# Moving the S5 preparation of a hybrid trunk kernel to VectorE: broadcast products in pieces behind the weight splits

## The chip, the cores and the metric

The kernel runs on one core of one Trainium2 chip. The metric is the device time of one execution in microseconds (us); the kernel before takes 1494.66 us, the median of three runs. A core has five engines that run their own queues of instructions: TensorE (PE in the profile) multiplies matrices, VectorE (DVE) and GpSimd (POOL) work elementwise, ScalarE (ACT) applies functions and copies, and SyncE (SP) issues the transfers (DMA).

## The reference

`reference.py` computes two layers on 272 tokens (16 learned ones and 256 of x) with 1024 features, all in float32. What matters here is the frame and head group D, the S5 state space:

```python
for l in range(DEPTH):
    h = h + 0.5 * swiglu(rms_norm(h, ffn1_norm[l]), ffn1_w_gate[l], ffn1_w_up[l], ffn1_w_down[l])
    h = h + hybrid_mixer(rms_norm(h, mix_norm[l]), w_in[l], w_out[l], lru_p, gdn_p, ssd_p, s5_p)
    h = h + 0.5 * swiglu(rms_norm(h, ffn2_norm[l]), ffn2_w_gate[l], ffn2_w_up[l], ffn2_w_down[l])
return rms_norm(h, final_norm)[:, N_META:]
...
def s5_mixer(u, a_re, a_im, log_dt, b_re, b_im, c_re, c_im, d_skip, w_glu, norm_g):
    mag = jnp.exp(dt * lam_re)
    ab_re = mag * jnp.cos(dt * lam_im)
    ab_im = mag * jnp.sin(dt * lam_im)
    f_re = ((ab_re - 1.0) * lam_re + ab_im * lam_im) / den
    f_im = (ab_im * lam_re - (ab_re - 1.0) * lam_im) / den
    bb_re = f_re[..., None] * b_re - f_im[..., None] * b_im
    bb_im = f_re[..., None] * b_im + f_im[..., None] * b_re
    bu_re = jnp.einsum("btgi,gpi->tbgp", ug, bb_re)
    ...
    _, _, s_re, s_im = lax.associative_scan(_complex_linear_combine, ...)
    y = jnp.einsum("tbgp,gip->btgi", s_re, c_re) - jnp.einsum("tbgp,gip->btgi", s_im, c_im)
```

Everything that depends on a, b, c and log_dt alone (no token) can be prepared ahead of the mixing sub-layer. That is the S5 preparation of which this document tells.

## The kernel before

**Stages.** Each layer is FFN1, mixing, FFN2. Activations have features on partitions and tokens on the free axis. The weights come in 382 chunks of 128 x 1024 numbers, 191 a layer: 66 for FFN1 (44 for gate and up, 22 for down), 59 for mixing, 66 for FFN2.

**A chunk's way.** SyncE loads it into `raw` (RAWS = 3 buffers); ScalarE makes its upper part `hi` (L214) and VectorE the lower part `lo` = raw - hi (L216; in mixing every fourth one on GpSimd); TensorE uses it in 24 matmuls, for each of eight 128 x 128 tiles hi x, hi x_lo and lo x (L227, L228, L229). `ahead` keeps AHEAD = 3 chunks split ahead of the one in use, in SPLITS = 4 buffers. In an FFN's gate and up part VectorE also does three operations of 128 x 272 for every two chunks (L353, L355, L358).

**What sets the order.** The program is written step by step, and a scheduler orders each engine's instructions by a simulated timeline in which code written earlier has priority, so that work whose inputs are there moves forward. An engine then executes its queue strictly in order.

**The S5 preparation.** The 16 pairs of S5 groups are treated in four quarters u of four pairs. `d_consts` makes the small arrays of both layers (a, its powers `pw`, the factor f). `d_powers(l, u)` multiplies b and c with f and the powers of a, as complex products `cmul` of 128 x 128 elements on GpSimd: eight products of six operations a quarter, and two more operations. `d_mats(l, u)` then makes four matrices with TensorE and ScalarE (transposes, F, H) and, on VectorE, tables of a ** (4 j) of 68 columns, in seven doubling steps of six small operations a quarter; all goes to DRAM (`spill`), and `d_load` brings it back in the mixing sub-layer. The scratch of `cmul` appears in the trace as dp (GpSimd) and cx (VectorE), the quarter's arrays as s5a, s5b, dU, du, rx and rg.

**Where it is called.** `run` gives each layer's FFN1 a table of hooks: after gate and up tile f = 1, 3, 7, 12, 16, 20 of 22 the quarters' powers and matrices; in layer 0, `mix_consts`, `a_consts` and `d_consts` (constants of the mixers, many small VectorE operations) come first, at f = 1. The second FFN has no hooks. As the powers of layer 1 depend on parameters alone, the scheduler moves them forward.

## Time and profile before

| | us |
|---|---|
| three runs | 1494.46, 1494.66, 1499.1 |
| median | 1494.66 |
| span of the profiled execution | 1506.5 |
| TensorE busy in it | 1407.3 |
| VectorE busy | 1078.3 |
| ScalarE busy | 698.3 |
| GpSimd busy | 536.1 |

The profiled execution is another one than the three that are timed; the page prints its span, from the first instruction to the last, and no time of its own beside it. Layer 0 has its FFN1 at about 12 to 244 us of the span, its mixing until about 570 and its FFN2 from about 605 to 800; layer 1 follows with FFN1 until about 1005, mixing until 1305 and FFN2 until 1495. PEclk is the granted TensorE clock, as a share of full speed.

### The profile page before, as it was taken

What the parts mean: (1) busy time and instruction counts of PE and PEld (TensorE: products, weight loads), DVE (VectorE), ACT (ScalarE), POOL (GpSimd) and SP (SyncE); (2) the same over time, 40 slices, a digit from 0 to 9 for tenths busy, and PEclk for the clock granted to TensorE, in tenths of its full rate; (3) what the DMA queues carried; (4) which work ended last, traced back from release to release, by engine and by line L of the source; (5) the groups of instructions that cost most, each with busy time, mean ns of one, the idle gap of its engine ahead of it and who ended that gap; (6) DMA issues with size and microseconds to landing.
All of it is one profiled execution on the core that took longest, in us unless ns stands there. A gap on an engine that the chain in (4) does not pass through costs nothing.

```text
span 1506.5 us, 28168 instructions
## 1 busy us (share of the span) xinstructions
PE 1407.3 (93%) x10838; PEld 1366.9 (91%) x10838; DVE 1078.3 (72%) x2078; ACT 698.3 (46%) x1169; POOL 536.1 (36%) x779
## 2 busy tenths in 40 slices
PE   7988999989898995999999999999898899999997
PEld 6987998979897895999999999998898879999997
DVE  8998666888987469556565876667898875666653
ACT  5435444444563342444444455443355633554442
POOL 2589312265544588000010660122564344200011
PEclk9999999989999997999999999999899989999998
DMA  6456664654422153555555667646454222565562
GB/s 222 149 192 210 235 227 139 203 192 114 134 78 90 43 170 107 185 169 178 173 179 159 201 206 252 210 137 209 137 172 134 85 85 70 165 199 184 185 188 88
DMA packets 85197, 243.18 MB, mean 161 GB/s; under 512 B 22968, under 2 KB 29896, under 8 KB 85064
## 3 DMA queue, kind: packets, MB, share of 16 engines
q1 hardware_dynamic: 85064, 241.38, 49.7%
q8 instruction: 86, 1.41, 0.4%
q14 instruction: 47, 0.39, 0.1%
HBM read 221.86 MB, written 19.49 MB: 160 GB/s over the span
## 4 chain that ended last, share of the span: by engine, by line
PE 65%; DVE 10%; POOL 2%; DMA 2%; issue 2%; ACT 1%; SPq 0%; DVEq 0%; ACTq 0%; POOLq 0%
PE g L227 18%; PE g L228 18%; PE g L229 18%; DVE lo L216 2%; PE m L664 2%; PE m L235 1%; PE m L257 1%; PE m L1143 1%; PE m L797 1%; DVE r L875 1%; DVE r L543 1%; PE m L1107 1%; DVE r L1112 1%; POOL lo L216 1%; DMA a<-scr 1%
## 5 line engine op out<-in xcount | busy, mean ns | idle before, releaser
L227 PE MATMUL g<-xh,hi 128*128 128x272 f32 (+1 forms) x2048 | 601.4, 294 | 46.2 <-DVE r L543 16.3
L214 ACT ACTIVATE hi<-raw 128x1024 fp32r<-128x1024 f32 (+1 forms) x382 | 402.4, 1054 | 471.1 <-PE g L228 230.3
L229 PE MATMUL g<-xh,lo 128*128 128x272 f32 (+1 forms) x2048 | 599.5, 294 | 14.2 <-DVE lo L216 14.1
L228 PE MATMUL g<-xl,hi 128*128 128x272 f32 (+1 forms) x2048 | 597.9, 293 | 1.4 <-DVE xl L312 1.4
L216 DVE TENSOR_TENSOR lo<-raw,hi 128x1024 fp32r<-128x1024 f32 (+1 forms) x352 | 454.1, 1290 | 202.5 <-ACT hi L214 199.9
L227 PEld LDWEIGHTS g<-xh,hi 128*128 128x128 f32 x2048 | 394.7, 193 | 49.0 <-issue 17.5
L229 PEld LDWEIGHTS g<-xh,lo 128*128 128x128 f32 x2048 | 393.8, 193 | 18.0 <-DVE lo L216 17.4
L228 PEld LDWEIGHTS g<-xl,hi 128*128 128x128 f32 x2048 | 394.6, 193 | 2.8 <-DVE xl L312 1.8
L272 POOL TENSOR_TENSOR acc<-acc,r 128x272 f32<-128x272 f32 (+1 forms) x42 | 44.2, 1052 | 515.7 <-ACT r L271 515.0
L216 POOL TENSOR_TENSOR lo<-raw,hi 128x1024 fp32r<-128x1024 f32 x30 | 74.5, 2482 | 82.7 <-ACT hi L214 82.6
L228 PE MATMUL g<-r,hi 128*128 128x272 f32 (+1 forms) x256 | 73.0, 285 | 0.0
L355 DVE TENSOR_TENSOR r<-r,g 128x272 f32<-128x272 f32 (+1 forms) x88 | 37.7, 429 | 36.7 <-PE g L229 34.9
L354 ACT ACTIVATE r<-r 128x272 f32<-128x272 f32 (+1 forms) x88 | 36.6, 416 | 46.4 <-DVE r L353 46.3
L229 PE MATMUL g<-ra,lo 128*128 128x272 f32 (+1 forms) x192 | 55.1, 287 | 0.0
L229 PE MATMUL g<-rq,lo 128*128 128x272 f32 (+1 forms) x192 | 55.0, 289 | 0.0
L227 PE MATMUL g<-ra,hi 128*128 128x272 f32 (+1 forms) x192 | 54.9, 286 | 0.0
L228 PE MATMUL g<-rs,hi 128*128 128x272 f32 (+1 forms) x192 | 54.9, 286 | 0.0
L228 PE MATMUL g<-rz,hi 128*128 128x272 f32 (+1 forms) x192 | 54.8, 285 | 0.0
L227 PE MATMUL g<-rq,hi 128*128 128x272 f32 (+1 forms) x192 | 53.8, 291 | 0.0
L353 DVE TENSOR_TENSOR r<-g,rstd 128x272 f32<-128x272 f32 (+1 forms) x88 | 38.0, 431 | 21.0 <-PE g L229 20.9
L249 POOL TENSOR_TENSOR toks<-tok,mhalf 128x2 f32<-128x2 f32 (+1 forms) x36 | 26.6, 752 | 70.9 <-DVE tok L246 65.1
L228 PEld LDWEIGHTS g<-r,hi 128*128 128x128 f32 x256 | 48.3, 189 | 0.0
(439 smaller groups left out, 2873.3 us busy)
## 6 DMA issues: line engine op xcount, KB each, us to landing
raw<-in_wgu_dram SPq DMA_DIRECT2D x176, 512.0 KB, 4.1
raw<-in_wdn_dram SPq DMA_DIRECT2D x88, 512.0 KB, 4.2
raw<-in_win_dram SPq DMA_DIRECT2D x80, 512.0 KB, 3.6
raw<-in_wout_dram SPq DMA_DIRECT2D x32, 512.0 KB, 3.5
spill<-s5a SPq DMA_DIRECT2D x8, 920.0 KB, 5.3
s5a<-spill SPq DMA_DIRECT2D x8, 920.0 KB, 4.7
s5b<-spill SPq DMA_DIRECT2D x8, 896.0 KB, 4.8
spill<-rx SPq DMA_DIRECT2D x4, 640.0 KB, 3.5
```

The costliest lines, as they stand in the source:

```text
L214: nc.scalar.activation(out=hi[:, 0:w], in_=raw[:, 0:w], func=AF.Copy)
L216: (nc.gpsimd if mixing and i % 4 == 1 else nc.vector).tensor_tensor(out=lo[:, 0:w], in0=raw[:, 0:w], in1=hi[:, 0:w].bitcast(F32), op=ALU.s ...
L227: nc.tensor.matmul(ps, lhsT=hi, rhs=xh, start=start, stop=False)
L228: nc.tensor.matmul(ps, lhsT=hi, rhs=xl, start=False, stop=False)
L229: nc.tensor.matmul(ps, lhsT=lo, rhs=xh, start=False, stop=stop)
L235: s.nc.tensor.matmul(ps[0:w, c + b * st:c + b * st + 1], lhsT=acc[:, o:o + w], rhs=s.ones[:, 0:1], start=True, stop=True)
L249: nc.gpsimd.tensor_tensor(out=rs[0:w, b0:b1], in0=tok[0:w, b0:b1], in1=s.mhalf[0:w, 0:1].to_broadcast([w, b1 - b0]), op=ALU.pow)
L272: (eng or nc.gpsimd).tensor_tensor(out=acc, in0=acc, in1=t, op=ALU.add)
L353: nc.vector.tensor_tensor(out=t, in0=g[:, t0], in1=r, op=ALU.mult)
L354: nc.scalar.activation(out=si, in_=t, func=AF.Silu)
L355: nc.vector.tensor_tensor(out=a, in0=si, in1=u[:, t0], op=ALU.mult)
L664: s.nc.tensor.matmul(ps[:, h * 128:h * 128 + 128], lhsT=lhs(h), rhs=rhs(h), start=True, stop=True)
```

## The change

The preparation becomes a generator, `d_prep(l)`, that yields after each small piece. `ahead` asks for one piece behind each weight split outside of mixing (from chunk 4 on), and the scheduler is told to place it behind that split. In layer 0's FFN1 the pieces are those of `d_consts`, `d_prep(0)`, `mix_consts` and `a_consts`, about 63 for 62 splits; `d_prep(1)` has 44 pieces, behind the splits of layer 0's FFN2, and layer 1's FFN1 has none. The rest, if any, is issued at the end of the FFN by `finish_work`.

In `d_prep`, the tables are made for all 16 pairs at once (seven steps of six operations of 16 to 512 columns a layer, in place of four times as many of 4 to 256). The products with b and c are four `twice` a quarter, each two products and a sum of 128 x 512 elements whose operands are broadcast: the powers of a up to the fourth come from a table `aux` that `d_consts` makes for both layers, of which layer 1's part waits in DRAM (`auxd`). All these are on VectorE; GpSimd keeps memsets. ScalarE takes over the copy of m4 and two copies into W. The tables are stored to DRAM apart, in eight small stores a layer, and their place in the quarter's array changes. The 8 transposes and 8 small matmuls of a quarter stay. The diff also drops comments, which moves line numbers.

```diff
@@ ahead
-            (nc.gpsimd if mixing and i % 4 == 1 else nc.vector).tensor_tensor(out=lo[:, 0:w], in0=raw[:, 0:w], in1=hi[:, 0:w].bitcast(F32), op=ALU.subtract)
+            ins = (nc.gpsimd if mixing and i % 4 == 1 else nc.vector).tensor_tensor(out=lo[:, 0:w], in0=raw[:, 0:w], in1=hi[:, 0:w].bitcast(F32), op=ALU.subtract)
             s.split.append((hi, lo))
+            if not mixing and i >= 4:
+                with s.tc.issue_after(ins.ins):
+                    next(s.work, None)
@@ ffn
-            for k in hooks.get(f, ()):
-                k()
@@ d_consts: many lines
...
+        for k in (3, 4):
+            rot(A(0, k), A(1, k), A(0, 2), A(1, 2), A(0, k - 2), A(1, k - 2))
+        yield
+        for k in (1, 2, 3):
+            rot(Fp(0, k), Fp(1, k), fr, fi, A(0, k), A(1, k))
...
+        nc.scalar.activation(out=s.aux, in_=aux[:, 0], func=AF.Copy)
+        nc.sync.dma_start(out=s.auxd, in_=aux[:, 1])
@@ cmul, d_powers and d_mats go
...
+    def twice(s, o, a, c, b, d, op, pat, **k):
+        v = s.nc.vector
...
+        t = s.pt(n).rearrange(pat, **k)
+        v.tensor_tensor(out=o, in0=a, in1=c, op=ALU.mult)
+        v.tensor_tensor(out=t, in0=b, in1=d, op=ALU.mult)
+        if n > 256:
+            yield
+        v.tensor_tensor(out=o, in0=o, in1=t, op=op)
+
+    def d_prep(s, l):
...
+        if l:
+            nc.sync.dma_start(out=s.aux, in_=s.auxd)
...
         for k in range(7):
             n = 1 << k
             m = min(n, NC4 - n)
...
+            yield from s.twice(tr[:, :, n:n + m], a, c, b, d, sub, 'p (q c) -> p q c', q=NQ)
+            if m > 4:
+                yield
+            yield from s.twice(ti[:, :, n:n + m], a, d, b, c, add, 'p (q c) -> p q c', q=NQ)
+            yield
+        for u in range(4):
...
+            for r, t in enumerate((tr, ti)):
+                nc.sync.dma_start(out=sp[:, 1296 + 272 * r:1568 + 272 * r], in_=t[:, qs, :].rearrange('p q c -> p (q c)'))
+            raw = s.buf('bc', [P, 4, 4, 32])
+            nc.sync.dma_start(out=raw, in_=s.ap['s5b'][l, u])
...
+            nc.scalar.activation(out=m4, in_=s.m4[:, l, qs].unsqueeze(2).to_broadcast([P, 4, NC4]), func=AF.Copy)
...
+            yield from s.twice(B[:, 0], over(0), fr, over(1), fi, sub, 'p (q k c) -> p q k c', **pat)
+            yield
+            yield from s.twice(B[:, 1], over(0), fi, over(1), fr, add, 'p (q k c) -> p q k c', **pat)
...
+            yield from s.twice(W[:, 0, :, 1:5], over(2), ar, over(3), ai, sub, 'p (q k c) -> p q k c', **pat)
+            yield
+            yield from s.twice(W[:, 1, :, 1:5], over(2), an, over(3), ar, sub, 'p (q k c) -> p q k c', **pat)
...
+    def first_work(s):
+        yield from s.d_consts()
+        yield from s.d_prep(0)
+        s.mix_consts()
+        yield
+        s.a_consts()
@@ run
-            hooks = {1: [lambda: s.d_powers(l, 0)], 3: [lambda: s.d_powers(l, 1)], 7: [lambda: s.d_mats(l, 0), lambda: s.d_powers(l, 2)],
-                     12: [lambda: s.d_mats(l, 1), lambda: s.d_powers(l, 3)], 16: [lambda: s.d_mats(l, 2)], 20: [lambda: s.d_mats(l, 3)]}
             if l == 0:
-                hooks[1] = [s.mix_consts, s.a_consts, s.d_consts] + hooks[1]
-            s.ffn(l, full, lambda m: s.norm_in(m, s.col('nm', l), full), hooks, l == 0)
+                s.work = s.first_work()
+            s.ffn(l, full, lambda m: s.norm_in(m, s.col('nm', l), full), l == 0)
+            s.finish_work()
...
+                s.work = s.d_prep(l + 1)
                 s.ffn(l, sl, lambda m: s.norm_in(m, s.col('n1', l + 1), sl))
+                s.finish_work()
```

**VectorE in layer 0's FFN1.** The rows are VectorE's queue in the gate and up part; lo is a weight split, r the FFN's activations, s5a the quarter's tables with their scratch cx, pw the powers of a, rx the products with c, rg the loaded b and c. Before:

```order
L1014 TENSOR_TENSOR cx_1078<-s5a_1045,pw 128x4x16
L1017 TENSOR_TENSOR cx_1078<-s5a_1045,pw 128x4x16
L914 TENSOR_TENSOR pw<-pw,a_72 128x32
L353 TENSOR_TENSOR r_1239<-g_1177,rstd 128x272
L914 TENSOR_TENSOR a_72<-pw 128x32
L914 TENSOR_TENSOR pw<-pw 128x32
L1013 TENSOR_TENSOR cx_1078<-s5a_1045,pw 128x4x16
L1018 TENSOR_TENSOR cx_1078<-s5a_1045,pw 128x4x16
L914 TENSOR_TENSOR pw<-pw,a_72 128x32
L1015 TENSOR_TENSOR s5a_1045<-cx_1078 128x4x16
L216 TENSOR_TENSOR lo_1236<-raw_1031,hi_1235 128x1024
L1019 TENSOR_TENSOR s5a_1045<-cx_1078 128x4x16
```

After the change:

```order
L217 TENSOR_TENSOR lo_1612<-raw_1520,hi_1611 128x1024
L1047 TENSOR_TENSOR rx_395<-rg_1444,aux 128x4x128
L1048 TENSOR_TENSOR cx_976<-rg_1444,aux 128x512
L360 TENSOR_TENSOR r_1621<-r_1620,g_1584 128x272
L217 TENSOR_TENSOR lo_1655<-raw_1561,hi_1654 128x1024
L1051 TENSOR_TENSOR rx_395<-rx_395,cx_976 128x4x128
L363 TENSOR_TENSOR r_1460<-r_1621,ra_1298 128x272
L358 TENSOR_TENSOR r_1692<-g_1627,rstd 128x272
L217 TENSOR_TENSOR lo_1687<-raw_1609,hi_1686 128x1024
L1047 TENSOR_TENSOR rx_395<-rg_1444,aux 128x4x128
```

The runs of small table operations between two splits are gone from here; behind each split stands one piece, two products of 128 x 512 or the sum of them.

**VectorE where layer 0's FFN2 begins.** The rows stand around the sums for the norm (tok); lo_6748 and lo_6531 are splits of the FFN's first chunks. Before, the tables of layer 1's first quarters stand here:

```order
L1017 TENSOR_TENSOR cx_9630<-s5a_9597,pw 128x4x32
L1018 TENSOR_TENSOR cx_9630<-s5a_9597,pw 128x4x32
L1015 TENSOR_TENSOR s5a_9597<-cx_9630 128x4x32
L246 TENSOR_SCALAR tok_6674<-m_6670 128x2
L246 TENSOR_SCALAR tok_6674<-m_6670 16x1
L1019 TENSOR_TENSOR s5a_9597<-cx_9630 128x4x32
L1013 TENSOR_TENSOR cx_9630<-s5a_9597,pw 128x4x4
L1014 TENSOR_TENSOR cx_9630<-s5a_9597,pw 128x4x4
L216 TENSOR_TENSOR lo_6748<-raw_6594,hi_6747 128x1024
L1017 TENSOR_TENSOR cx_9630<-s5a_9597,pw 128x4x4
L1018 TENSOR_TENSOR cx_9630<-s5a_9597,pw 128x4x4
L1015 TENSOR_TENSOR s5a_9597<-cx_9630 128x4x4
```

After the change:

```order
L1048 TENSOR_TENSOR cx_6406<-dz_973,aux 128x16
L302 SCALAR_TENSOR_TENSOR xl<-h,small,xh 128x272 x2
L1051 TENSOR_TENSOR dp_972<-dp_972,cx_6406 128x16
L277 TENSOR_TENSOR acc<-acc,r_6394 128x272
L1051 TENSOR_TENSOR dz_973<-dz_973,cx_6406 128x16
L251 TENSOR_SCALAR tok_6457<-m_6453 128x2
L251 TENSOR_SCALAR tok_6457<-m_6453 16x1
L217 TENSOR_TENSOR lo_6531<-raw_6367,hi_6530 128x1024
L1047 TENSOR_TENSOR dp_972<-dp_972,aux 128x16x2
L1048 TENSOR_TENSOR cx_6406<-dz_973,aux 128x32
L1047 TENSOR_TENSOR dz_973<-dp_972,aux 128x16x2
L1048 TENSOR_TENSOR cx_6406<-dz_973,aux 128x32
L1051 TENSOR_TENSOR dp_972<-dp_972,cx_6406 128x16x2
```

Here stand now the first pieces of `d_prep(1)`, whose tables are dp (real) and dz (imaginary).

**GpSimd at the end of layer 0's mixing.** The rows stand around the last sums of squares acc of the residual, which the norm ahead of FFN2 needs. Before, the powers of layer 1 (dp and rx, with abr and abi) stand between them:

```order
L1014 TENSOR_TENSOR dp_519<-rx_544,abr 128x4x32
L1013 TENSOR_TENSOR dp_519<-rx_544,abi 128x4x32
L272 TENSOR_TENSOR acc<-acc,r_6603 128x272
L1017 TENSOR_TENSOR dp_519<-rx_544,abr 128x4x32
L1018 TENSOR_TENSOR dp_519<-rx_544,abi 128x4x32
L1015 TENSOR_TENSOR rx_544<-dp_519 128x4x32
L272 TENSOR_TENSOR acc<-acc,r_6609 128x272
L1019 TENSOR_TENSOR rx_544<-dp_519 128x4x32
L1014 TENSOR_TENSOR dp_519<-rx_544,abr 128x4x32
L272 TENSOR_TENSOR acc<-acc,r_6615 128x272
L1013 TENSOR_TENSOR dp_519<-rx_544,abi 128x4x32
```

After the change:

```order
L217 TENSOR_TENSOR lo_6310<-raw_6247,hi_6309 128x1024
L1086 MEMSET s5b_6917 128x512
L1088 MEMSET s5a_6916 128x4
L277 TENSOR_TENSOR acc<-acc,r_6376 128x272
L277 TENSOR_TENSOR acc<-acc,r_6382 128x272
L277 TENSOR_TENSOR acc<-acc,r_6388 128x272
L254 TENSOR_TENSOR toks_6458<-tok_6457,mhalf 128x2
L254 TENSOR_TENSOR toks_6458<-tok_6457,mhalf 16x1
L1140 MEMSET dz_973 128x4 x2
L1088 MEMSET s5a_7252 128x4
```

GpSimd has memsets and the norm's own operations here.

## Rows read from the trace of the kernel before

**Rows 1.** The page: span, then busy time, share and count by engine.
```profile
span 1506.5 us, 28168 instructions
...
PE 1407.3 (93%) x10838; PEld 1366.9 (91%) x10838; DVE 1078.3 (72%) x2078; ACT 698.3 (46%) x1169; POOL 536.1 (36%) x779
```
**Rows 2.** Stretches of 40 us: length, busy time by engine, clock, DMA, GB/s.
```profile
40.00:80.00 40.00, 37.72 (x300) 37.25 (x299) 39.36 (x140) 17.00 (x25) 26.74 (x55) 1.00 0.46 145
80.00:120.00 40.00, 36.36 (x281) 35.04 (x280) 34.95 (x92) 19.26 (x34) 35.75 (x70) 1.00 0.64 217
120.00:160.00 40.00, 33.49 (x262) 32.56 (x261) 33.85 (x95) 17.18 (x28) 40.00 (x75) 1.00 0.56 187
160.00:200.00 40.00, 38.88 (x311) 38.44 (x310) 25.85 (x54) 20.19 (x31) 2.71 (x5) 1.00 0.75 264
200.00:240.00 40.00, 40.00 (x322) 40.00 (x321) 26.43 (x31) 18.95 (x25) 5.17 (x6) 1.00 0.61 198
560.00:600.00 40.00, 22.39 (x147) 21.21 (x145) 37.17 (x60) 11.14 (x18) 36.89 (x78) 0.79 0.34 116
600.00:640.00 40.00, 39.98 (x303) 39.98 (x304) 24.49 (x36) 18.92 (x29) 0.00 (x0) 0.95 0.58 185
880.00:920.00 40.00, 38.91 (x312) 38.69 (x311) 32.73 (x106) 18.91 (x30) 15.04 (x28) 1.00 0.59 192
```
**Rows 3.** Waits of TensorE from 40 to 180 us: us in total, times, longest.
```profile
PE g L229 <- DVE lo L216: 11.2, 11, 3.0
```
**Rows 4.** VectorE's timeline, layer 0's FFN1, GpSimd busy: start, us, instruction.
```profile
101.24 0.38 DVE L1017 TENSOR_TENSOR cx<-s5a,pw 128x32 f32<-128x32 f32 x1
101.55 0.18 DVE L1018 TENSOR_TENSOR cx<-s5a,pw 128x32 f32<-128x32 f32 x1
101.65 0.45 DVE L1015 TENSOR_TENSOR s5a<-cx 128x32 f32<-128x32 f32 x1
```
**Rows 5.** VectorE's timeline, prices: tables, a split, and products of 128 x 512.
```profile
576.96 0.28 DVE L1018 TENSOR_TENSOR cx<-s5a,pw 128x128 f32<-128x128 f32 x1
577.16 0.28 DVE L1015 TENSOR_TENSOR s5a<-cx 128x128 f32<-128x128 f32 x1
...
577.90 1.20 DVE L216 TENSOR_TENSOR lo<-raw,hi 128x1024 fp32r<-128x1024 f32 x1
579.04 0.38 DVE L1017 TENSOR_TENSOR cx<-s5a,pw 128x16 f32<-128x16 f32 x1
...
1159.67 0.69 DVE L674 TENSOR_TENSOR r<-a,cst 128x512 f32<-128x512 f32 x1 [0.47 <-DMA a<-s]
1160.28 0.68 DVE L674 TENSOR_TENSOR rk<-a,cst 128x512 f32<-128x512 f32 x1
...
599.54 0.42 DVE L355 TENSOR_TENSOR r<-r,g 128x272 f32<-128x272 f32 x1
599.89 0.43 DVE L353 TENSOR_TENSOR r<-g,rstd 128x272 f32<-128x272 f32 x1
```
**Rows 6.** Timeline of VectorE and GpSimd where layer 0's FFN2 begins.
```profile
583.99 15.63 DVE L216 TENSOR_TENSOR lo<-raw,hi 128x1024 fp32r<-128x1024 f32 x1 [0.36 <-ACT hi L214]
...
584.99 0.45 POOL L1015 TENSOR_TENSOR dU<-dp 128x128 f32<-128x128 f32 x1
```
**Rows 7.** Waits of TensorE, 560 to 610 us, columns as in group 3.
```profile
PE g L227 <- DVE r L355: 11.6, 1, 11.6
PE g L227 <- DVE r L353: 3.0, 1, 3.0
PE m L235 <- DVE acc L272: 2.6, 1, 2.6
```
**Rows 8.** TensorE's timeline at the start: its first wait for a split.
```profile
11.23 0.59 PE L229 MATMUL g<-xh,lo 128*128 128x272 f32 x1 [1.82 <-DVE lo L216]
```
**Rows 9.** DMA issues: count, KB each, median us to landing; VectorE's wait.
```profile
rg<-in_s5b_dram SPq DMA_DIRECT2D x8, 256.0 KB, 3.8
...
DVE s5a L1064 <- DMA spill<-s5a: 12.7, 3, 5.0
```

More of the change, by code (lines that the diff above doesn't have):

```diff
@@ L136, in __init__ @@
         s.now = {}
+        s.work = iter(())
         s.a3 = s.const([P, 1408], 'a3')
@@ L340, in first_tiles, with ffn @@
         return pss
-    def ffn(s, l, sl, done, hooks={}, whole=False):
+    def ffn(s, l, sl, done, whole=False):
         nc = s.nc
@@ L960, in rot @@
             tt(os, os, t, add)
+        yield
         rot(co, si, cs, sn, C, S)
-        s.abr, s.abi, s.fr, s.fi, s.m4 = (K(t) for t in ('abr', 'abi', 'fr', 'fi', 'm4'))
-        tt(s.abr, mg, co, mul)
-        tt(s.abi, mg, si, mul)
+        yield
+        abr, abi, fr, fi = A(0, 1), A(1, 1), Fp(0, 0), Fp(1, 0)
+        tt(abr, mg, co, mul)
+        tt(abi, mg, si, mul)
         d, t2, t3, am = y('sd'), y('st2'), y('st3'), y('am')
@@ L982, in d_consts @@
         rot(a, b, co, si, co, si)
-        rot(s.pw[:, 0, 0], s.pw[:, 0, 1], a, b, a, b)
+        rot(pw(0, 0), pw(0, 1), a, b, a, b)
+        yield
         for k in range(6):
-            a, b = s.pw[:, k, 0], s.pw[:, k, 1]
-            rot(s.pw[:, k + 1, 0], s.pw[:, k + 1, 1], a, b, a, b)
+            a, b = pw(k, 0), pw(k, 1)
+            rot(pw(k + 1, 0), pw(k + 1, 1), a, b, a, b)
+            yield
+        v.memset(A(0, 0), 1.0)
+        v.memset(A(1, 0), 0.0)
+        rot(A(0, 2), A(1, 2), abr, abi, abr, abi)
+        for k in (3, 4):
+            rot(A(0, k), A(1, k), A(0, 2), A(1, 2), A(0, k - 2), A(1, k - 2))
+        yield
+        for k in (1, 2, 3):
+            rot(Fp(0, k), Fp(1, k), fr, fi, A(0, k), A(1, k))
+        for k in range(4):
+            ts(X(512 + k * NQ), A(1, k + 1), -1.0, mul)
+        nc.scalar.activation(out=s.aux, in_=aux[:, 0], func=AF.Copy)
+        nc.sync.dma_start(out=s.auxd, in_=aux[:, 1])
+        yield
         s.spill = [[s.dp.tile([P, 3632], F32, name=f'spill{l}{u}', tag=f'spill{l}{u}') for u in range(4)] for l in range(L)]
@@ new lines, in pt @@
+    def pt(s, n):
+        s.turn ^= 1
+        return s.buf('pt', [P, 1024])[:, 512 * s.turn:512 * s.turn + n]
+    def twice(s, o, a, c, b, d, op, pat, **k):
+        v = s.nc.vector
+        n = 1
+        for x in o.shape[1:]:
+            n *= x
+        t = s.pt(n).rearrange(pat, **k)
+        v.tensor_tensor(out=o, in0=a, in1=c, op=ALU.mult)
+        v.tensor_tensor(out=t, in0=b, in1=d, op=ALU.mult)
+        if n > 256:
+            yield
+        v.tensor_tensor(out=o, in0=o, in1=t, op=op)
@@ new lines, in d_prep @@
+    def d_prep(s, l):
+        nc = s.nc
+        sub, add = ALU.subtract, ALU.add
+        if l:
+            nc.sync.dma_start(out=s.aux, in_=s.auxd)
+        pw = s.aux[:, 0:224].rearrange('p (k r q) -> p k r q', k=7, r=2)
+        ap_, fp_ = s.aux[:, 224:384].rearrange('p (r k q) -> p r k q', r=2, k=5), s.aux[:, 384:512].rearrange('p (r k q) -> p r k q', r=2, k=4)
+        an_ = s.aux[:, 512:576].rearrange('p (k q) -> p k q', k=4)
+        tr, ti = (s.buf(n, [P, NQ, NC4]) for n in ('tre', 'tim'))
+        nc.gpsimd.memset(tr[:, :, 0:1], 1.0)
+        nc.gpsimd.memset(ti[:, :, 0:1], 0.0)
@@ L1068, in d_mats @@
             m = min(n, NC4 - n)
-            c, d = (s.pw[:, k, r, l, qs].unsqueeze(2).to_broadcast([P, 4, m]) for r in range(2))
-            s.cmul(v, tb[:, 0, :, n:n + m], tb[:, 1, :, n:n + m], tb[:, 0, :, 0:m], tb[:, 1, :, 0:m], c, d)
-        v.tensor_copy(out=m4, in_=s.m4[:, l, qs].unsqueeze(2).to_broadcast([P, 4, NC4]))
-        v.memset(m4[:, :, 0:1], 0.0)
-        sp = s.spill[l][u]
-        nc.sync.dma_start(out=sp[:, 0:1840], in_=ta)
-        nc.sync.dma_start(out=sp[:, 1840:3120], in_=W.rearrange('p r q t c -> p (r q t c)'))
@@ L1278, in mixing, with finish_work @@
                 do[name](*a)
+    def first_work(s):
+        yield from s.d_consts()
+        yield from s.d_prep(0)
+        s.mix_consts()
+        yield
+        s.a_consts()
+    def finish_work(s):
+        for _ in s.work:
+            pass
     def run(s):
```

120 lines of the change are left out of this document (55 added, 65 removed).

## The prediction, made before the changed kernel ran

> **What bounds the kernel now.** I read the page's busy times first [rows 1]. TensorE is busy 93% of the 1506.5 us span, so the path is TensorE's own work and whatever makes it wait. VectorE with 72% looks safe, but that is a mean over stages, so I went on to stretches of 40 us [rows 2]. The last stretch of layer 0's FFN1 (200:240) is the measure: 322 matmuls in 40 us, 0.124 us each, without a gap, and VectorE busy only 26.43. The four stretches before it have 300, 281, 262 and 311. They lack 22 + 41 + 60 + 11 = 134 matmuls, 134 x 0.124 = **16.6 us**. There VectorE is at 39.36, 34.95 and 33.85 us of 40, and GpSimd is full too, at 26.74, 35.75 and 40.00. The list of TensorE's waits names the cause: 11 waits for VectorE's split `lo`, 11.2 us in all [rows 3].
>
> Why is VectorE so full? Its timeline there [rows 4] shows tiny table operations that take far more than their size: of two products with the same 128x32, one starts 0.31 us before its successor, the other 0.10. GpSimd runs products in the same time. In a moment without a GpSimd operation a four times larger one (128x128) needs 0.20 from start to start [rows 5].
>
> The second place is the step from mixing to FFN2 in layer 0. The stretches 560:600 and 600:640 have 147 and 303 matmuls in place of 644 [rows 2]: 194 lost, 24.1 us. TensorE waits 11.6, 3.0 and 2.6 us for VectorE there [rows 7]. The 11.6 have one source: a weight split that lasts 15.63 us instead of 1.20 [rows 5, 6], while GpSimd executes the powers of layer 1, one after the other at up to 0.45 us. The clock that is low after this idle time, 0.95 in 600:640, means 4 of its 40 us at half speed, or 2.0 us of work lost. So the long split cost 13.6, and other losses there 24.1 - 13.6 = **10.5 us**.
>
> **How the profiled execution stands to the median.** Its span is 1506.5, and the median run 1494.66, so this execution is a slow sample. 1506.5 - 13.6 = 1492.9 is 1.8 below the median, which can well lie around a span. I take it that the timed runs do not hold the long split and base the sum on 1492.9 + 1.8 = 1494.7. That they do hold it is a rival below.
>
> **What the change costs on VectorE.** A split takes 1.14 from start to start, a product of 128x512 0.60, an FFN operation of 128x272 0.35 [rows 5]. No row of before has exactly the new operands; the cheapest bound for such a product is half a split (0.57), as it has half the columns, the dearest a whole split (1.14). The row of 128x512 also has a broadcast operand in its code's line, and so I take 0.60.
> - Added a layer: 16 `twice` of three operations, 48 x 0.60 = 28.8 us. The tables for all pairs are 7 steps of 6 operations of 16 to 512 columns; by 0.10 at 32 columns or fewer [rows 4], 0.20 at 128 and 0.60 at 512, and what lies between on a line, 6 x 1.59 = 9.5 us. Together 38.3.
> - Removed a layer: the quarters' tables, 4 x 42 operations of 4 to 256 columns, by the same prices 6 x 0.83 x 4 = 20 us uncontended, and on GpSimd 8 x 6 x 4 = 192 operations of products and 8 copies.
> So VectorE gets 18 us more of its own work. What it loses is company: GpSimd keeps no product in an FFN but the sums of squares.
>
> Per chunk in layer 0's FFN1: TensorE gives 24 x 0.124 = 2.98 us. VectorE has 1.14 for the split, 1.5 operations of 0.35 for the FFN, together 1.67, and one piece. The tables, products and constants (38 us, and 15 for some 150 tiny operations of 0.10) over 62 slots make 0.85 on average, 2.5 in all; the worst piece is two products, 1.2, hence 2.87. It fits, narrowly, and with three chunks ahead a single late split costs nothing. Where the cover goes, each us beyond 2.98 a chunk is a us on the path.
>
> **The sum.**
> 1. Layer 0's FFN1: of 16.6 I leave 3.0, about a fifth, as the worst piece is 96% of a chunk and ScalarE and GpSimd still have work of their own: **-13.6** (bounds -16.6 and 0).
> 2. Mixing to FFN2 in layer 0: GpSimd's products no longer stand between the last sums of squares, and VectorE's tables no longer ahead of FFN2's splits; small tables of `d_prep(1)` take their place. Of 10.5 I keep 1: **-9.5** (bounds -10.5 and 0).
> 3. Layer 1's FFN1: it loses its hooks; 880:920 lacks 10 matmuls [rows 2], **-1.2** (bounds -1.2 and 0).
> 4. Start: TensorE waits 1.82 us for a split [rows 8], behind small constant operations that now come later: **-1.0** (bounds -1.8 and 0).
> 5. Layer 0's FFN2 gets 38.3 us on VectorE, which is busy 24.49 of 40 in 600:640 [rows 2], so 0.6 to 0.8 of its 190 us. Covered; I allow **+1.5** (0 to 5).
> 6. FFN1 to mixing in layer 0: the last constants, some 70 tiny operations (7 us), now stand in the last four chunks, and the last quarter's stores and the first reload come ahead of weight loads on SyncE: **+1.5** (0 to 6).
> ScalarE's 27 more copies (46% busy [rows 1]) and the eight small stores a layer I cost at nothing: ScalarE's cover is the 1.9 of 2.98 us that a chunk's `hi` leaves. The transposes and matmuls of the preparation stay.
> Sum: -13.6 - 9.5 - 1.2 - 1.0 + 1.5 + 1.5 = -22.3, and 1494.7 - 22.3 = **1472.4 us**.
>
> Why should GpSimd's going free VectorE? The rows have a tiny operation at 0.31 us beside a GpSimd operation where 0.10 is its price [rows 4], and a split that lasts 15.63 - 1.20 = 14.4 us too long beside many, none above 0.45 us [rows 6]; both go if GpSimd's products do. The Trainium skill, "SBUF — State Buffer", section "Who interferes with whom", states that a VectorE instruction with two SBUF inputs contends with a GpSimd instruction that reads SBUF, for a shared port that is held for a whole instruction. It agrees in kind with the first row; by that rule taken alone a split would wait for one GpSimd operation, 0.45 us, not for 14.4, the long split would be something else and could return in an execution, and that execution would take 1472.4 + 13.6 = 1486 us.
>
> **Rivals.**
> - *VectorE stays tight.* Half of the FFN1's loss (8.3 where I leave 3.0) and half of the transition's (5 where I leave 1) stay: 1472.4 + 5.3 + 4 = about **1482**. For it: 2.87 of 2.98. Against: three chunks of slack.
> - *The timed runs hold the long split too*, and the profile is slow for another reason: 13.6 more to win, **1459**. For it: it is a normal instruction's wait in the program's order. Against: the 11.8 us between span and median, so close to 13.6.
> - *Nothing is won.* The extra 18 us on VectorE eat what the contention gave in FFN1 (16.6 stays lost, not 3.0), and the first pieces of `d_prep(1)` hold FFN2's splits as the tables did (10.5 stays, not 1): 1472.4 + 13.6 + 9.5 = **1495.5**. For it: how little VectorE has over by the mean. Against: 200:240 without a gap, where GpSimd has 5.17 us [rows 2].
> - *The long split is not GpSimd's doing* and comes back in some executions: 1472.4 + 13.6 = **1486** where it does. For it: 14.4 us beside operations of 0.45 [rows 6]. Against: no such split where GpSimd has no products.
> - *The pieces wait at VectorE's head (slower).* Each quarter's b and c load is issued behind weight loads and after the last reading of the one buffer, about two chunks, 6 us, ahead of its first product; the load takes 3.8 us, and VectorE has waited for the quarter's stores up to 5.0 us before [rows 9]. A piece that waits holds the splits behind it. Up to two chunks of split work are ahead, so TensorE waits once a load lands more than about 11 us after its issue. With 4 us in each of eight quarters: 1472.4 + 32 = **1504**. Against: 3.8 is far from 11.
>
> **How the numbers follow.** Chances: the forecast 0.57, tight 0.17, the long split too 0.12, nothing won 0.06, the long split back 0.03, the wait at the head 0.05. A measurement of this kernel can tell about 0.3%, 4.5 us. Faster: the first three and the long split back, with a little taken off for unforeseen costs, 0.88; the same: nothing won, 0.06; slower: the wait at the head and what nothing won has above, 0.06. The range runs from 1458 (the long split in the timed runs) to 1486 (tight, with its terms 5 and 6 at 3 to 4 each); beyond lie nothing won, the wait at the head and the tails of the others, under 0.2.
>
> **What would show it.** In the changed profile 40:200 should have near 322 matmuls in each stretch, the waits for `lo` there should fall from 11.2 to a few us, VectorE's products show 0.60 from start to start, and the stretch where layer 0's FFN2 begins has no split beyond 1.3 us and some 90% of 644 matmuls. FFN2 of layer 0 shows VectorE at about 32 of 40 without waits of TensorE. The prediction is wrong if the products cost near 1.1 (then 48 of them overfill their chunks), if waits for `lo` go on in FFN1 or appear in layer 0's FFN2, or if VectorE shows waits for DMA on a product.

## The result, and the profile after

The changed kernel takes 1460.12 us, the median of four runs (1455.58 to 1469.81), against 1496.88 of before (four runs, 1494.46 to 1507.96). The two medians differ by 36.8 us; the ratio of the fast runs, which is not the quotient of these medians, is 0.9731, with a 95% interval of 0.9688 to 0.9775, or some 40 us. The forecast of 1472.4 stood for a ratio of 0.985: direction and places were right, the size too small by 15 to 18 us.

The page of the changed kernel, span and busy times, to be read beside [rows 1]:

```profile
span 1460.6 us, 27660 instructions
...
PE 1392.4 (95%) x10838; PEld 1357.4 (93%) x10838; DVE 1057.2 (72%) x1932; ACT 710.1 (49%) x1194; POOL 335.0 (23%) x391
```

TensorE has the same 10838 instructions. GpSimd lost 201 us of busy time, and VectorE, which took over its work, is still 21 us less busy than before. The forecast gave it some 18 us a layer more of its own work, so more than that came back in shorter instructions.

The stretches of 40 us of the changed kernel, columns as in [rows 2]; the last two hold the step from mixing to FFN2 of layer 0, which comes earlier now:

```profile
40.00:80.00 40.00, 40.00 (x319) 40.00 (x318) 36.16 (x140) 19.01 (x29) 0.54 (x3) 1.00 0.56 178
80.00:120.00 40.00, 40.00 (x321) 40.00 (x320) 36.57 (x83) 21.06 (x33) 0.22 (x2) 1.00 0.69 211
120.00:160.00 40.00, 40.00 (x324) 40.00 (x324) 30.66 (x46) 21.91 (x38) 0.74 (x3) 1.00 0.74 238
160.00:200.00 40.00, 40.00 (x323) 40.00 (x322) 32.26 (x44) 24.65 (x39) 4.05 (x6) 1.00 0.68 213
200.00:240.00 40.00, 38.57 (x305) 37.90 (x304) 31.27 (x83) 17.11 (x28) 7.30 (x6) 1.00 0.65 223
540.00:580.00 40.00, 39.83 (x315) 39.42 (x314) 33.92 (x76) 21.21 (x33) 5.18 (x5) 1.00 0.55 171
580.00:620.00 40.00, 40.00 (x323) 40.00 (x322) 32.21 (x54) 22.87 (x37) 0.85 (x4) 1.00 0.74 233
```

From 40 to 200 us TensorE now has 319, 321, 324 and 323 matmuls where it had 300, 281, 262 and 311, and no wait of it is left there, where [rows 3] had 11. The step into FFN2 has 315 + 323 = 638 in place of 450 of 644. VectorE is at 36 of 40 us beside a TensorE without a gap: as full as before, and no longer in the way. The price of a piece is as forecast; VectorE's timeline shows operations of 128x512 0.60 us from start to start, first of the tables, then of the products with b and c (du), and a split at 1.21:

```profile
96.29 0.68 DVE L1048 TENSOR_TENSOR cx<-dz,aux 128x512 f32<-128x512 f32 x1
96.89 0.68 DVE L1051 TENSOR_TENSOR dp<-dp,cx 128x512 f32<-128x512 f32 x1
97.50 0.43 DVE L363 TENSOR_TENSOR rz<-r,ra 128x272 fp32r<-128x272 f32 x1
97.85 0.43 DVE L358 TENSOR_TENSOR r<-g,rstd 128x272 f32<-128x272 f32 x1
98.20 1.21 DVE L217 TENSOR_TENSOR lo<-raw,hi 128x1024 fp32r<-128x1024 f32 x1
...
590.93 0.68 DVE L1047 TENSOR_TENSOR du<-rg,aux 128x512 f32<-128x512 f32 x1
591.53 0.69 DVE L1048 TENSOR_TENSOR cx<-rg,aux 128x512 f32<-128x512 f32 x1
```

To see where the time came from I took, in each trace, the start of the same matmuls (counting only those with 272 or 256 columns, of which every kernel has 9312), and so the length of the same piece of the program. `again` is a second profile (e1 and e8 below); e9 is the kernel before without any products.

| us, from matmul to matmul | before | before again | after | after again | e9 |
|---|---|---|---|---|---|
| start (0 to 300) | 45.7 | 45.3 | 43.6 | 42.9 | 45.7 |
| layer 0's FFN1 (300 to 1650) | 198.3 | 203.2 | 183.5 | 183.1 | 180.7 |
| its mixing (1650 to 3000) | 300.0 | 299.5 | 299.3 | 298.5 | 296.0 |
| the step into FFN2 (3000 to 3300) | 62.9 | 62.9 | 39.8 | 39.8 | 39.9 |
| FFN2 (3300 to 4650) | 169.7 | 169.7 | 180.8 | 180.8 | 169.8 |
| layer 1's FFN1 (4650 to 6300) | 221.8 | 220.9 | 210.3 | 210.3 | 220.4 |
| its mixing (6300 to 7650) | 290.5 | 278.7 | 284.5 | 284.1 | 284.4 |
| its FFN2 (7650 to 9311) | 197.3 | 197.3 | 197.3 | 197.3 | 197.3 |

Two places pay: layer 0's FFN1 with 15 to 20 us and the step into its FFN2 with 23.1. That FFN2 grows by 11.1 and layer 1's FFN1 shrinks by 10.6 to 11.5 is TensorE's own work of layer 1's preparation, which moved from the one to the other. In the second pair the stages add to 40.7 us, near the difference of the times. In the first pair they add to 47.1, of which 6.0 stand in layer 1's mixing, where e8 finds scatter.

### The profile page after: what moved, and what is told of

The parts are those of the page before. It is cut to its first block, busy times and chain, and to the rows that moved or that the text cites. A ratio compares the mean times of both kernels' runs of the same rounds, so it can differ in the third digit from the quotient of the medians.

```text
span 1460.6 us, 27660 instructions
## 1 busy us (share of the span) xinstructions
PE 1392.4 (95%) x10838; PEld 1357.4 (93%) x10838; DVE 1057.2 (72%) x1932; ACT 710.1 (49%) x1194; POOL 335.0 (23%) x391
## 4 chain that ended last, share of the span: by engine, by line
PE 67%; DVE 9%; DMA 2%; issue 2%; POOL 1%; ACT 1%; SPq 0%; DVEq 0%; ACTq 0%; POOLq 0%
PE g L232 19%; PE g L233 19%; PE g L234 19%; PE m L667 2%; DVE lo L217 2%; PE m L240 1%; PE m L262 1%; DVE s5a L877 1%; DMA raw<-in_win_dram 1%; PE m L800 1%; DVE r L1160 1%; DVE r L546 1%; PE m L1191 1%; DVE r L878 1%; DMA a<-scr 1%
## 5 line engine op out<-in xcount | busy, mean ns | idle before, releaser
L217 DVE TENSOR_TENSOR lo<-raw,hi 128x1024 fp32r<-128x1024 f32 (+1 forms) x352 | 435.3, 1237 | 211.1 <-ACT hi L215 207.8
L217 POOL TENSOR_TENSOR lo<-raw,hi 128x1024 fp32r<-128x1024 f32 x30 | 74.0, 2468 | 88.0 <-ACT hi L215 87.6
L553 ACT ACTIVATE r<-r 128x272 f32<-128x272 f32 x40 | 17.2, 429 | 63.4 <-DVE r L547 46.4
L546 DVE SCALAR_TENSOR_TENSOR r<-g,small,r 128x269 f32<-128x269 f32 x80 | 39.2, 490 | 11.9 <-ACT r L543 11.0
```

What stands on the lines that cost most here:

```text
L217: ins = (nc.gpsimd if mixing and i % 4 == 1 else nc.vector).tensor_tensor(out=lo[:, 0:w], in0=raw[:, 0:w], in1=hi[:, 0:w].bitcast(F32), op ...
L546: nc.vector.scalar_tensor_tensor(out=dst[:, o:T], in0=ps[:, 0:T - o], scalar=taps[:, j:j + 1], in1=dst[:, o:T], op0=ALU.mult, op1=ALU.add)
L553: nc.scalar.activation(out=t, in_=x, func=AF.Tanh, scale=0.5)
```

## The experiments

Theory: VectorE lost its time beside GpSimd's products, and that is the whole gain. Rivals: VectorE's own many small table operations were the cause, or the placing of the pieces. The times are medians, and each run of the kernel before that goes with them was on the same chip; e1 to e4 share 1499.88 us (23 runs), e5 to e8 1503.55 (17), e9 to e12 1503.07 (11). Across these three groups only ratios compare. Line numbers shift with each edit: the split is L214 to L217, and a product of cmul L1013 to L1024, by run.

**e1: the changed kernel again**, no edit.

> The changed kernel once more, for the size of the gain and for what differs between executions. If the first result's 36 us is typical: a ratio of 0.973 to 0.978 (1456 to 1462 us). If the forecast's sum was right and the first four runs were lucky: about 0.985 (1472). The profile is to show again no wait for a split in layer 0's FFN1 and no loss where its FFN2 begins; the part of the gain in layer 1's mixing (about 6 us in the first profile, of which no term of the sum told) should stay if the change makes it, and be gone or another if it is scatter.

1457.69 us, ratio 0.9722 (0.9667 to 0.9777). The size stands. No wait from 40 to 180 us, the step at 39.8 again. Layer 1's mixing took 284.1.

**e8: the kernel before again**, no edit, one run.

> The kernel before, a second profile. If the 6 us by which layer 1's mixing is shorter in the first profile after is the change's doing, this stretch takes 290 us again; if it is scatter between executions, 280 to 285 as in the three variants of before. A long split where layer 0's FFN2 begins may be there or not: 13 to 15 us in the first profile.

1500.65 us, and a trace with a long split at the same place. VectorE's timeline, and the last product of GpSimd's run beside it:

```profile
588.69 15.62 DVE L216 TENSOR_TENSOR lo<-raw,hi 128x1024 fp32r<-128x1024 f32 x1 [0.38 <-ACT hi L214]
...
602.83 0.39 POOL L1018 TENSOR_TENSOR dp<-rg,fi 128x128 f32<-128x128 f32 x1
```

It lasts 15.62 us, where the first profile had 15.63 [rows 6]. GpSimd's run ends at 603.22 and the split at 604.31, so the split gets 1.1 us of its own after it. What differs most between the two profiles is layer 1's mixing. Its stretch in the first, then in the second (columns as in [rows 2]):

```profile
1007.00:1297.00 290.00, 267.04 (x1964) 251.22 (x1963) 226.62 (x427) 140.17 (x279) 131.83 (x149) 0.93 0.42 129
```
```profile
1011.00:1290.00 279.00, 258.72 (x1969) 243.88 (x1969) 226.02 (x427) 140.94 (x278) 133.47 (x149) 0.97 0.43 135
```

The same work, 290.5 - 278.7 = 11.8 us longer in the first, with a granted clock of 0.93 where the second has 0.97, and one wait of TensorE of 6.9 us where the second has 4.3. So what put the first profile's span above the median lies here, and not in the long split. What the wait of 6.9 us is for (L543) stands behind a VectorE copy of 16x12 that took 3.22 us beside a GpSimd split, and another copy of 4.08 follows; the second profile has 0.27 and 0.20.

```profile
1060.88 3.22 DVE L487 COPY g<-ghr 16x12 f32<-16x12 f32 x1
1063.15 0.95 DVE L543 SCALAR_TENSOR_TENSOR r<-g,small,r 128x269 f32<-128x269 f32 x1
1064.16 4.08 DVE L488 COPY g<-tokv 16x12 f32<-16x12 f32 x1
```

In the other runs this stretch takes 279 to 288 us, with 284 in the changed kernel; no change shows here. Layer 0's FFN1, in turn, is 4.9 us longer in the second profile, behind a held copy (last section).

**e2: GpSimd's products of layer 1 late, the tables in their places.** The kernel before, with

```diff
-                nc.gpsimd.tensor_tensor(out=rs[0:w, b0:b1], in0=tok[0:w, b0:b1], ...)
+                s.lastg = nc.gpsimd.tensor_tensor(out=rs[0:w, b0:b1], in0=tok[0:w, b0:b1], ...)
...
+                if l == 1 and kind in LATE:
+                    with s.tc.issue_after(s.lastg.ins if kind == 'powers' else s.last.ins):
+                        k()
...
```

Here `LATE = ('powers',)`: layer 1's `d_powers` stand behind `lastg`, the last power of the norm on GpSimd; with `'mats'` its `d_mats` would stand behind `last`, the last split.

> The kernel before, in which layer 1's products on GpSimd may not move ahead of layer 1's own FFN1 (they stand behind its norm); VectorE's tables stay where they were, some of them where layer 0's FFN2 begins. Theory (GpSimd's products are what slows VectorE and holds the norm): the long split is gone in every execution, and of the other 10.5 us lost between mixing and FFN2 of layer 0 at least 7 come back; but the products now run beside the tables in layer 1's FFN1, which loses 8 to 15 us in place of 1.2. In all 1486 to 1496. Rival (VectorE's own tables stand ahead of the first splits and of the norm): the step into FFN2 still loses 8 to 10 us beside the long split, and layer 1's FFN1 loses as before, near 1 us.

1505.91 us, ratio 1.0036 (1.0003 to 1.0069). The step into FFN2 takes 40.3 us in place of 62.9: the products' leaving gives 22.6 of the 23.1 back, the 10.5 too, though the tables stayed. But layer 1's FFN1 takes 245.8 where the kernel before has 221.8, 24 us more and not 8 to 15, so the time missed the theory's 1486 to 1496. VectorE's split and GpSimd's last product there:

```profile
800.46 26.48 DVE L217 TENSOR_TENSOR lo<-raw,hi 128x1024 fp32r<-128x1024 f32 x1 [0.57 <-ACT hi L215]
...
825.46 0.39 POOL L1023 TENSOR_TENSOR dp<-rg,fi 128x128 f32<-128x128 f32 x1
```

The long split went with the products, to 26.48 us, and ended 1.1 us after GpSimd's run, which has no gap from 776.82 to 825.85 and 68 operations beside the split.

**e3: the tables late, GpSimd's products in their places.** The same edit, with `LATE = ('mats',)`.

> The kernel before, in which layer 1's tables and matrices on VectorE stand behind a split of layer 1's FFN1, while GpSimd's products run early as before. Theory (GpSimd): the step from mixing to FFN2 still loses 15 to 24 us, with waits for the norm and, in some executions, a split of many us beside the products; time 1490 to 1500. Rival (tables): the step loses 5 us or less beside the long split, and the time falls to about 1484.

1491.69 us, ratio 0.9969 (0.9928 to 1.001): the theory's time, which the interval does not tell from the kernel before, but not its place. The step takes 44.4, so 18.5 of the 23.1 come back here too. A long split is there:

```profile
599.84 8.93 DVE L217 TENSOR_TENSOR lo<-raw,hi 128x1024 fp32r<-128x1024 f32 x1 [0.46 <-ACT hi L215]
...
607.30 0.39 POOL L1023 TENSOR_TENSOR dp<-rg,fi 128x128 f32<-128x128 f32 x1
```

But TensorE waited only 0.7 us for it: it was held for 8.93 us, and the splits before it had been made in time. Why it was held for less time than the 15 us of before is not settled; the run of products may just have been nearer its end. So products beside a split are not enough for the loss of before; the tables, which stand ahead of the splits at the step, add to it. That so little of the 18.5 shows in the time is in part the other stages of this execution: layer 0's FFN1 took 204.6 us and layer 1's 225.2, 6.3 and 3.4 more than in the first profile.

**e4: layer 0's products left out.** The kernel before; W and B hold zeros in layer 0.

```diff
-        s.cmul(g, B[:, 0, :, 3], B[:, 1, :, 3], raw[:, 0], raw[:, 1], sc(s.fr), sc(s.fi))
-        for j in (2, 1, 0):
+        if l == 0:
+            g.memset(B, 0.0)
+        else:
+            s.cmul(g, B[:, 0, :, 3], B[:, 1, :, 3], raw[:, 0], raw[:, 1], sc(s.fr), sc(s.fi))
+        for j in (2, 1, 0) if l else ():
...
```

> The kernel before, in which layer 0's 192 product operations on GpSimd are left out (memsets stand for their results, so the output is not the reference's); VectorE's tables and constants stay as they are. Theory (a VectorE operation is slowed by GpSimd's products): the matmuls missing from 40 to 200 us fall from 134 (16.6 us) to 25 or fewer (3 us), VectorE's busy time there falls by some 30 us, and the time falls by 12 to 16 us. Rival (VectorE has too many small operations of its own): 80 or more stay missing, and the time falls by 6 us or less.

1480.61 us, 0.9864 (0.9815 to 0.9914), 20 us less: a little over the theory's 12 to 16. Layer 0's FFN1 takes 180.7 us, no matmul is missing from 40 to 200 us, and TensorE's waits from 40 to 250 us are three, 2.8 us in all, and none for a split. VectorE's busy time from 40 to 200 us fell by 17.4 us, from 134.0 to 116.6, and not by 30. The step into FFN2 keeps its 63.2, with a split locked out for 15.7 us.

**e9: all products left out.** As e4, in both layers.

> The kernel before with the products on GpSimd left out in both layers (memsets in their place, so the output is not the reference's); the tables, the constants and all places on VectorE stay as before. Theory (all of the gain is GpSimd's products being gone from beside VectorE): layer 0's FFN1 takes 181 us, the step into FFN2 40 to 43 and the time is 1456 to 1464, as the changed kernel, though nothing of the tables is merged or placed. Rival (merging the tables and placing the pieces behind splits brings a part): 1470 or more, with the step into FFN2 above 48 us.

1461.37 us, 0.9735 (0.969 to 0.978), the changed kernel's time. Two of its stretches:

```profile
120.00:160.00 40.00, 40.00 (x325) 40.00 (x325) 25.59 (x75) 21.93 (x36) 0.53 (x1) 1.00 0.65 213
...
540.00:580.00 40.00, 39.88 (x315) 39.42 (x314) 29.61 (x80) 21.51 (x33) 4.50 (x5) 1.00 0.52 168
```

The tables and constants are what they were, in quarters, in bulk, where they stood, and TensorE has 325 matmuls where it had 262. So GpSimd's products account for a loss as large as the gain, and the tables need not be merged or placed to win it back. But VectorE has nothing of the products' work here. What the broadcast form and the places are worth once VectorE does that work, e9 cannot tell; e10 and e12 can.

**e12: the old products on VectorE.** The kernel before with one word changed.

```diff
     def d_powers(s, l, u):
-        g = s.nc.gpsimd
+        g = s.nc.vector
```

> The kernel before with one change, its complex products of 128x128 as they are but on VectorE (192 operations and 8 copies a layer, 0.20 us each by the profile, some 39 us a layer), with no pieces and no broadcast form. Theory (what counts is that GpSimd reads nothing beside VectorE): no split over 2 us, and the time is 1460 to 1474, most of the gain. Rival (VectorE has no room for them without the broadcast form and the placing): waits for splits of 20 us or more in all, 1485 or above.

1467.69 us, 0.976 (0.972 to 0.9799): as the theory had it. This line alone brings some 35 us; VectorE has room for 39 us a layer more. Against e11, a form of the changed kernel on the same chip with 1454.56 us and 0.9678 (0.9643 to 0.9714), 13 us are lacking, and the intervals do not touch. The traces have most of them at the step, 45.1 us against 39.3, and in layer 0's mixing, 302.7 against 298.9. At the step one power of the norm on GpSimd takes 5.96 us, where it takes 0.71 in the changed kernel, and TensorE waits 2.6 us for it, as in e10. Why mixing is longer is open.

**e6: the broadcast products on GpSimd.** The changed kernel, with

```diff
-        v = s.nc.vector
...
+        v = s.nc.gpsimd if 'k' in k else s.nc.vector
```

> The changed kernel with its broadcast products (48 operations of 128x512 a layer) on GpSimd, where nothing holds them behind a split, so that they come early; tables, pieces and places on VectorE stay. Theory (company of GpSimd is what costs): layer 0's FFN1 or FFN2 show splits of 5 us and more beside the products, and the time is 1470 to 1490. Rival (fewer and larger operations are what helped, wherever they run): 1455 to 1464 as the changed kernel, as VectorE has 29 us a layer less to do.

1473.2 us, 0.9804 (0.9756 to 0.9852): the theory's time, without its long splits; the longest takes 2.31 us. VectorE and GpSimd slow each other in turns instead. GpSimd's and VectorE's timelines:

```profile
141.41 1.08 POOL L1048 TENSOR_TENSOR cx<-rg,aux 128x512 f32<-128x512 f32 x1
142.44 3.31 POOL L1047 TENSOR_TENSOR rx<-rg,aux 128x512 f32<-128x512 f32 x2
...
143.50 1.31 DVE L363 TENSOR_TENSOR r<-r,rn 128x272 fp32r<-128x272 f32 x1
144.74 0.43 DVE L358 TENSOR_TENSOR r<-g,rstd 128x272 f32<-128x272 f32 x1
145.09 1.75 DVE L217 TENSOR_TENSOR lo<-raw,hi 128x1024 fp32r<-128x1024 f32 x1
```

An operation of 0.43 us takes 1.31, a split of 1.21 takes 1.75. Layer 0's FFN1 is at 192.0 us, 9 more than the changed kernel, FFN2 at 184.4, 4 more.

**e5: GpSimd's chain broken by memsets.** The kernel before, with zeros written over the scratch ahead of each half of a complex product.

```diff
+        if g is s.nc.gpsimd:
+            g.memset(p[:, s.turn, :, 0:n], 0.0)
         return p[:, s.turn, :, 0:n], p[:, s.turn + 1, :, 0:n]
```

> The kernel before, in which GpSimd writes zeros over a scratch array twice within each complex product (128 more operations, which read nothing), so that no more than about four products that read follow each other. In three profiles a split that began beside GpSimd's products ended 1.1 us after GpSimd's unbroken run of products did. Theory (a split that has lost to GpSimd gets in only when GpSimd stops reading): no split lasts more than about 4 us any more, the executions scatter less, and the median falls from 1499.9 to 1484 to 1494, though GpSimd has some 25 us more to do. Rival (the long split has another cause, or only an idle GpSimd lets it go): splits of 8 us and more are still there, and the median stays at 1497 to 1505.

1499.73 us, 1.0005 (0.9967 to 1.0043): my theory of the lock fell, the rival stands. VectorE's longest instruction at the step, now an FFN operation, and GpSimd's queue near its end:

```profile
588.38 17.35 DVE L358 TENSOR_TENSOR rn<-r,rq 128x272 fp32r<-128x272 f32 x1
...
604.15 0.20 POOL L1008 MEMSET dp<- 128x128 f32 x1
604.32 0.39 POOL L1020 TENSOR_TENSOR dp<-rg,fi 128x128 f32<-128x128 f32 x1
604.68 0.39 POOL L1015 TENSOR_TENSOR dp<-rg,fi 128x128 f32<-128x128 f32 x1
605.03 0.39 POOL L1019 TENSOR_TENSOR dp<-rg,fr 128x128 f32<-128x128 f32 x1
```

In the trace 55 operations of GpSimd, 14 memsets among them, pass it by, and it ends at 605.73, 0.3 us after GpSimd's last.

**e7: layer 1's pieces in its own FFN1.**

```diff
-            if l == 0:
-                s.work = s.first_work()
+            s.work = s.first_work() if l == 0 else s.d_prep(l)
...
-                s.work = s.d_prep(l + 1)
```

> The changed kernel with layer 1's pieces behind the splits of layer 1's own FFN1, in place of layer 0's second FFN. Theory (covered work costs nothing in either FFN): within 3 us of the changed kernel, 1455 to 1461, with the 11 us of TensorE's small matmuls moved from one FFN to the other. Rival (layer 0's FFN2 was chosen for a reason: next to layer 1's mixing the last stores and reloads get in the way): 4 us or more slower.

1460.45 us, 0.9734 (0.9683 to 0.9784): no difference from e1 that the intervals tell. FFN2 takes 170.2 and layer 1's FFN1 220.9, so 10.6 us of TensorE's work moved.

**e10: pieces not behind the splits.** The changed kernel without `with s.tc.issue_after(ins.ins):`.

> The changed kernel without the rule that a piece stands behind its split: the pieces are written at the same places but the scheduler may move them forward. Theory (with three chunks split ahead and no products on GpSimd the place of a piece hardly matters): within 4 us of the changed kernel, 1454 to 1462. Rival (the pieces' order behind the splits is what keeps TensorE fed): waits for a split come back in layer 0's FFN1 or where FFN2 begins, and the time is 1465 or more.

1468.2 us, 0.9773 (0.9739 to 0.9807), the rival's time by another mechanism. The interval overlaps with that of e1, on another chip; against e11, on the same chip, it is 13.6 us slower and clear of it. Layer 0's FFN1 takes 181.5 us without a wait for a split. The step takes 46.8, in place of 39.8. GpSimd's, TensorE's and VectorE's timelines there:

```profile
554.99 8.21 POOL L253 TENSOR_TENSOR toks<-tok,mhalf 128x2 f32<-128x2 f32 x2 [5.05 <-DVE tok L250]
...
562.73 1.48 PE L261 MATMUL m<-cst,toks 128*128 128x128 f32 x5 [4.24 <-POOL toks L253]
...
560.90 1.21 DVE L217 TENSOR_TENSOR lo<-raw,hi 128x1024 fp32r<-128x1024 f32 x1
564.89 0.44 DVE L357 TENSOR_TENSOR r<-g,rstd 128x272 f32<-128x272 f32 x1 [2.78 <-ACT rstd L343]
```

Now GpSimd is the one that waits: the norm's two tiny powers take 8.21 us, the first alone 7.69 (0.71 in the changed kernel), while VectorE works through table pieces and splits without a pause until 562.11, and TensorE waits 4.24 us for them. In the changed kernel VectorE pauses for 2.60 us just ahead of the norm, and the pieces behind splits leave the powers room. Mixing of layer 0 is 5 us longer as well (304.0), for a reason that stays open.

**e11: pieces in bunches of ten.**

```diff
-            if not mixing and i >= 4:
+            if not mixing and i >= 4 and i % 10 == 4:
                 with s.tc.issue_after(ins.ins):
-                    next(s.work, None)
+                    for _ in range(10):
+                        next(s.work, None)
```

> The changed kernel with ten pieces behind every tenth split, in place of one behind each. Ten pieces hold up to 8 us of VectorE's work, less than the 9 us that three chunks split ahead give. Theory: 2 to 8 us slower than the changed kernel, with a few waits for a split of 1 to 3 us. Rival (the size of a piece is without effect): within 2 us.

1454.56 us, 0.9678 (0.9643 to 0.9714): the theory was wrong, and bunches cost nothing: no wait for a split from 40 to 260 us, and the step at 39.3. The interval overlaps with that of e1, on another chip, so nothing says that bunches are better.

## Why the prediction was right in its places and wrong in its size

**The step that failed** is the base. "I take it that the timed runs do not hold the long split" rested on 1506.5 - 13.6 being near the median. It was a coincidence: e8, with the same long split, takes 1500.65, and what made the first profile slow was layer 1's mixing, 11.8 us longer than in e8. The kernel before has this split in both of its profiles, e4 has it (15.71 us) with the same code at the step, and e5 has a hold of 17.35 us on another operation. Three timed runs were few as well: the medians of before beside the later runs are 1499.9, 1503.6 and 1503.1, with single runs from 1486 to 1514. So 13.6 us that I had taken out of the sum belong into the gain, and with them the sum would have said 35.9 us. What is then lacking, 1 to 6 us, is in terms 1, 4, 5 and 6 below. The forecast's own second rival, "the timed runs hold the long split too", said 1459; the first four runs gave 1460.12 and e1 1457.69. I gave it 0.12 on the strength of one agreement of two numbers. Whether the fastest runs of before (1486 to 1490) are without a long split stays open: timed runs leave no trace, and e1, which has no long split in its profile, spreads over 12 us too.

**The terms**, against the table:
1. Layer 0's FFN1, -13.6: measured -15 in the first pair and -20 in the second. Of the 3.0 that I left nothing stayed from 40 to 200 us, where the 16.6 were counted: 1287 of 1288 matmuls are there, and VectorE at 36 of 40 us costs TensorE nothing. The second profile of before lost 5 us more; there a copy of 128x272 took 5.83 us beside GpSimd (last section).
2. The step, -9.5 and, apart from the sum, -13.6: together 23.1, measured 23.1. GpSimd's products are the cause by e2 and e9, which give back 22.6 and 23.0; by e3, taking the tables away gives back 18.5 as well, so the two work together.
3. Layer 1's FFN1, -1.2, with term 5, FFN2 of layer 0, +1.5: measured together +0.5 in the second pair and -0.4 in the first, after the 11 us of TensorE's work that changed places. The pieces in FFN2 were covered; +1.5 was not needed.
4. Start, -1.0: measured -2.1 to -2.4.

Term 6, into mixing, +1.5: the mixing stretch became 0.7 to 1.0 us shorter. The constants' cost is there, though, a little ahead of it; among TensorE's waits from 180 to 250 us in the changed kernel is one for them. An operation of 128x8 ahead of it, of which the next one takes 0.15 us, took 2.15 and ended with a GpSimd split beside it:

```profile
PE g L232 <- DVE a L452: 1.2, 1, 1.2
...
227.57 2.15 DVE L451 TENSOR_TENSOR a<-a 128x8 f32<-128x8 f32 x1
...
227.33 2.38 POOL L217 TENSOR_TENSOR lo<-raw,hi 128x1024 fp32r<-128x1024 f32 x1 [4.37 <-ACT hi L215]
```

**Why GpSimd's going frees VectorE** was right, and e9 bears it out: with the products left out and all else in place, the kernel before is as fast as the changed one. What I weighed against it, that a split should wait for one GpSimd operation of 0.45 us at most, is refuted: in the first profile the split stayed out from 583.99 until GpSimd's run ended at 598.53, 39 operations long. The Trainium skill, "SBUF — State Buffer", section "SBUF: two separate sides", says that whichever of a VectorE instruction with two SBUF inputs and a GpSimd instruction that reads SBUF starts first gets the shared pair for the whole instruction, and the other fully blocks. The traces agree that one side stops, and show that it can stay stopped over many instructions of the other: 39 here.

Part of the gain may be another thing, GpSimd's own queue. TensorE waited 2.6 us at the step for the sums of squares [rows 7], which GpSimd makes between its products (VectorE's last sum waited 2.14 us for GpSimd's), and from 40 to 180 us 2.3 us for products themselves:

```profile
PE m L1059 <- POOL rx L1015: 1.8, 1, 1.8
PE m L1051 <- POOL du L1015: 0.5, 1, 0.5
```

The changed kernel and e9 have none of these waits. No run takes them away alone, so how much of the time they are worth is not shown.

**The other rivals.** VectorE did not stay tight, no piece waited at its head for a quarter's load, and something was won. The broadcast form and the pieces, which the change is named after, matter less than the engine, but they count: e12 with neither gains 35 us, and e11, which has both (with the pieces in bunches), 13 more on the same chip. Without the places e10 loses 7 us at the step, and 13.6 in its time against e11.

## What to carry to other kernels

Before taking a profile's odd instruction out of a sum as a rare event, look whether a second profile has it; a span that exceeds the median by the same amount proves nothing. Where an elementwise engine looks overfull, compare the same shape with and without work on the other engine beside it: here 39 us a layer more work on VectorE (e12) still left most of the gain, and 192 short products a layer on GpSimd cost some 40 us in both layers together (e9). Long unbroken queues of short operations on either of the two engines were the danger here, in both directions (e2 and e10), so look for them where the other engine has something that TensorE waits for.
